# First mixer of a two-layer decoder: the last slice of keys and queries, and the output gates, are made at other places of the recurrence

## The chip, the cores and the metric

The kernel runs on one core of one Trainium2 chip. The metric is device time in microseconds (us) for one execution of the whole program. The engines of the core are PE (matrix products and transposes), DVE, ACT and POOL (elementwise work), and SP, which only issues DMAs; POOL and ACT issue DMAs as well. Each engine works through its own instructions in order and waits on semaphores for the others.

## The reference, cut to what matters

One step of a two-layer decoder. The first layer is an mLSTM mixer over 1104 rows (64 sample rows, 16 meta rows, 1024 prompt rows), each of 1024 features. What the change touches is this mixer:

```python
p = xn @ w_in                        # queries, keys, values, output gate, input and forget gates
q, k, v = heads(p)                   # 8 heads, 64 wide for q and k, 128 wide for v
for chunk in chunks:                 # 9 chunks of rows: the 80 sample and meta rows, then 8 times 128
    s   = (q @ k.T) * exp(decay)
    num = w_inter * (q @ C) + s @ v
    den = w_inter * (q @ n) + sum(s)
    C, n = w_c * C + (w_g * k).T @ v, ...
h   = rmsnorm(num / max(|den|, exp(-m))) * mh_norm
out = (h * sigmoid(og)) @ w_out      # og: the output-gate columns of p
```

After the mixer come a SwiGLU block, the shared keys and values, a second mixer with attention, another SwiGLU block and the final norm. They aren't changed.

## The kernel before, in words

All products are made from two reduced-precision parts of each operand, so that each tile product is three matmuls (L266, L267, L268 in `mm3`). A weight block of 1024 x 128 is loaded raw (512 KB, SP's queue, L323), cast on ACT to its high part (`whi`, L336), and the low part (`wlo`) is the difference, on DVE (L337).

The 1104 rows are held in three slices of 336, 384 and 384 rows (x0, x1, x2; chunks 0-2, 3-5, 6-8). One weight block times one slice is a **unit**: eight **steps** of three matmuls each, into one PSUM bank `mmA` (two buffers). ACT then copies the bank to a staging tile `stg`, and POOL's queue writes it to a scratch tensor in device memory (`qkD` for keys and queries, `ogD` for the output gate).

The mixer, `phase_a`, runs in stages.

1. Values are projected for all rows.
2. `qk_out`: 8 weight blocks times 3 slices make queries and keys. Beside it `rec_prep` makes the decay terms on DVE and ACT; its few transposes on PE are put in after certain units (the ones of `stk` on L909 after the ninth).
3. `recurrence`: the chunks in order. The order of PE, DVE, ACT and POOL is the order of the code there (a manual schedule); SP's order is chosen by the compiler's scheduler. Chunk 0 (the sample rows, each with a state of its own) has many small products (`nps` L1164, `cs` L1213). Each later chunk i has: scores of chunk i+1 (`sps` L1077, `kps` L1083), state (`cp` L1116), decay of chunk i+2 (DVE L1061), outputs (`nps` L1176 and L1180, copied on ACT L1146), and sums of squares of its outputs (ACT L1198). After chunks 2, 5 and 8 `norm_heads` turns the sums into factors and scales the values in place (DVE L1256). A chunk's decay, keys and queries are loaded from scratch memory two chunks ahead (`chunk_load`, POOL's queue), into places that partly lie where chunk 0's states were.
4. Between these products `f(n)` puts n steps of filler on PE. The filler is `gates_out`: 8 weight blocks times 3 slices, 192 steps, whose result passes through a sigmoid on ACT (L741) on its way to `ogD`. What is left of it is emptied at the end of the pass for chunk 6. From then on the filler of chunks 7 and 8 is `gate`: load a gate tile of one head and slice, transpose the head's three value tiles on PE (`ghps` L1272), multiply by gain and gate on DVE (`yg` L1274), and split the product into its two parts (ACT L336, DVE L337). Ten of the 24 are made in the recurrence.
5. `mlp` goes on with the output weights: 8 blocks (`woraw` and `slot` on L520), the first four through one raw place. Then units of the output product (`pops`) alternate with the remaining 14 gates.

The memory of a core is filled from two sides. On the left lie the values, the recurrence's tiles, and the filler's weights; later the output weights lie there. On the right lie the ten `slots` of the feed-forward weights, of which the output weights use some.

Of the kernel before, what the change touches and what calls it, by code (L numbers as in the profile page):

```python
# [16 lines left out]
P = 128  # L17
# [232 lines left out]
class Net:  # L250
# [19 lines left out]
    def consts(self):  # L270
# [13 lines left out]
        self.clast = c.tile([P, 1], F32, name="clast")  # L284
        with self.pool("g0") as gp, self.pool("g0p", space=PSUM) as pp:
# [15 lines left out]
    def load_w(self, pieces, g=None, nk=KT, keep=None):  # L301
# [23 lines left out]
        if g is None:  # L325
# [144 lines left out]
    def mlp(self, H, w, l, heads=None, cb=None):  # L470
# [8 lines left out]
        with self.pool(self.uid("nsp")) as sp, self.pool(self.uid("npp"), bufs=2, space=PSUM) as pn:  # L479
# [26 lines left out]
            with ExitStack() as c:  # L506
# [6 lines left out]
                ws = []  # L513
                for m in range(KT):
# [11 lines left out]
                    self.split(raw, *ws[m])  # L526
                    t = m // 3
                    if m in (1, 4, 7) and (t == 0 or not heads):
                        load(nc.gpsimd if heads else nc.sync, t)

# [11 lines left out]
                if heads:  # L542
                    pad()
                    gate = heads(gp, c.enter_context(self.pool("ghp", bufs=2, space=PSUM)), "gh",
                                 lambda n: self.ny(n)[:, 0])
# [118 lines left out]
def phase_a(self, vt):  # L664
# [6 lines left out]
    with ExitStack() as c3:  # L671
# [29 lines left out]
        self.wpools(c3, 2, 3, side="left")  # L701
        self.cache_prep()

        def qk_out():

            for m in range(8):
                wh, wl = self.load_w([w_in[:, m * P : (m + 1) * P]])
                for t, (t0, t1) in enumerate(TS):
                    n = t1 - t0
                    ps = pp.tile([P, 512], F32, name=self.uid("mmA"), tag="mmA")  # L710
                    self.fm_cols(ps[:, :n], wh, wl, t)
                    s = st.tile([P, SL], F32, name=self.uid("stg"), tag="stg")
                    nc.scalar.activation(s[:, :n], ps[:, :n], AF.Copy, scale=DK ** -0.5 if m < 4 else 1.0)
                    nc.gpsimd.dma_start(qkD[m, :, t0:t1], s[:, :n])
# [10 lines left out]
        def gates_out():  # L725

            get = lambda m: self.load_w([w_in[:, (16 + m) * P : (17 + m) * P]])
            ws = [get(0)]
            for m in range(8):
                wh, wl = ws[m]  # L730
                for t, (t0, t1) in enumerate(TS):
                    n = t1 - t0
                    ps = pp.tile([P, 512], F32, name=self.uid("mmA"), tag="mmA")
                    xh, xl = self.X[t]
                    if t == 1 and m < 7:
                        ws.append(get(m + 1))
                    for k in range(KT):
                        self.mm3(ps[:, :n], wh[:, k, :], wl[:, k, :], xh[:, k, :], xl[:, k, :], k == 0, k == KT - 1)
                        if k == KT - 1:
                            s = st.tile([P, SL], F32, name=self.uid("stg"), tag="stg")  # L740
                            nc.scalar.activation(s[:, :n], ps[:, :n], AF.Sigmoid)  # L741
                            nc.gpsimd.dma_start(ogD[m, :, t0:t1], s[:, :n])
# [4 lines left out]
        def heads(gp, pp, tag="gh", op=None):  # L747
            ready = []
            todo = [(t, h) for t in (0, 1, 2) for h in left[t]]

            def ahead():
                if todo:
                    t, h = todo.pop(0)
                    og = op(self.uid("ogc"))
                    nc.gpsimd.dma_start(og[:, : TS[t][1] - TS[t][0]], ogD[h, :, TS[t][0] : TS[t][1]])
                    ready.append(og)

            def gate(t):
                if not left[t]:
                    return False  # L760
                if not ready:
                    ahead()
                ahead()
                self.gate_head(t, left[t].pop(0), v, ready.pop(0), gp, pp, tag)
                return True
            return gate

        self.recurrence(kp, self.rec, v, qkD, gates_out(), lambda gp: heads(gp, pp, "mmA", lambda n: st.tile([P, SL], F32, name=n, tag="stg")))
# [152 lines left out]
def recurrence(self, kp, rec, v, qkD, fill, gate):  # L921
# [4 lines left out]
    tm, den, ssq = self.fin  # L926

    def f(n):
        for _ in range(n):
            next(fill, None)  # L930

    C = [kp.tile([P, 4, DV + 1], F32, name=f"C{a}") for a in range(3)]
    E = mybir.EngineType
    with ExitStack() as cr, self.pool("recAp", bufs=2, space=PSUM) as pp, \
# [6 lines left out]
        with self.pool("sampA") as sp:  # L941
# [9 lines left out]
            f(2)  # L951
            self.first_sums(R, pp)
            f(3)
# [6 lines left out]
        with self.pool("rec2") as sets[2], self.pool("rec1", bufs=2) as rp, self.pool("rec3") as sets[0], \  # L960
                self.pool("gh0") as gp:
            R, N = N, load(2)
            f(10)
# [3 lines left out]
            g, norm = f, iter(())  # L967
            gate = gate(gp)
# [1640 lines left out]
```

## Time and profile before

| | us |
|---|---|
| median of 3 runs | 2934.68 |
| lowest, highest | 2930.90, 2948.07 |
| the profiled execution: its own time | 2934.39 |
| the profiled execution: span from first to last instruction | 2932.7 |
| PE busy in the span | 2820.7 |
| mean granted clock of PE | 0.988 |

A row of the profile names an engine, a line of the kernel, an operation and its tiles as out<-in; PEld is the loading of weights into PE, which overlaps PE. "Granted clock" is the share of full speed that the throttle allows PE. A row of waits reads: who waited for what, us in total, how often, the longest. In a row by stretch the columns are: start:end and length, then busy us and instructions of PE, PEld, DVE, ACT and POOL, then PE's granted clock, the DMA engines' share, and GB/s. All times of rows are counted from the start of the span.

### The profile page before, as it was taken

How to read it: one execution, taken by the hardware profiler on the slowest of the kernel's cores; microseconds unless marked ns; L12 is line 12 of the kernel's file. 1: busy time of each engine (PE TensorE's matmuls, PEld its weight loads, DVE VectorE, ACT ScalarE, POOL GpSimd, SP SyncE). 2: the span in 40 equal slices, each digit the busy share in tenths (PEclk: the TensorE clock that was granted, in tenths of full speed). 3: DMA queues.
4: the chain of work that ended last, by engine and by line, in shares of the span. 5: the costliest groups of instructions: out<-in, count | busy, mean ns of one | idle time of the engine just before them, and what ended most of it. 6: DMA issues, size and time to landing. Idle time of an engine off the chain costs nothing.

```text
span 2932.7 us, 53641 instructions
## 1 busy us (share of the span) xinstructions
PE 2820.7 (96%) x20542; PEld 2696.2 (92%) x20542; DVE 1704.8 (58%) x3406; ACT 1305.9 (45%) x2591; POOL 1002.1 (34%) x1480
## 2 busy tenths in 40 slices
PE   7999997999999999999999899999999999999998
PEld 7988887999999999999999887777899999999998
DVE  5032456687777755553355443677468777775543
ACT  5122354354444444442344453877444444443432
POOL 2021223156565511114353101454306565641110
PEclk9999998999999999999999999999999999999999
DMA  7052436222222276544443675443412222227652
GB/s 226 7 136 87 132 106 189 79 66 88 74 80 77 84 265 200 190 149 131 148 158 126 207 291 212 150 154 107 146 53 79 76 87 80 79 87 252 215 183 101
DMA packets 300139, 392.79 MB, mean 134 GB/s; under 512 B 32238, under 2 KB 222698, under 8 KB 298858
## 3 DMA queue, kind: packets, MB, share of 16 engines
q1 hardware_dynamic: 262978, 270.05, 28.8%
q0 software_dynamic: 33232, 117.01, 12.0%
q8 instruction: 161, 2.64, 0.4%
q10 hardware_dynamic: 3672, 2.31, 0.3%
q14 instruction: 96, 0.79, 0.1%
HBM read 292.19 MB, written 97.10 MB: 133 GB/s over the span
## 4 chain that ended last, share of the span: by engine, by line
PE 67%; DVE 11%; ACT 4%; issue 4%; DMA 2%; POOL 1%; DVEq 0%; ACTq 0%; POOLq 0%; SPq 0%
PE m L1331 23%; PE dps L266 6%; PE dps L267 6%; PE dps L268 6%; PE tmps L266 3%; PE tmps L267 3%; PE tmps L268 3%; PE sp L2396 1%; DVE slot L337 1%; PE pops L268 1%; PE op L2483 1%; PE pops L266 1%; PE pops L267 1%; DVE s L2400 1%; PE bps L266 1%
## 5 line engine op out<-in xcount | busy, mean ns | idle before, releaser
L337 DVE TENSOR_TENSOR slot<-slot,slot 128x1024 fp32r<-128x1024 f32 (+3 forms) x264 | 268.6, 1020 | 128.8 <-ACT slot L336 122.3
L336 ACT CAST slot<-slot 128x1024 fp32r<-128x1024 f32 (+3 forms) x264 | 207.8, 790 | 235.5 <-PE dps L267 92.0
L1331 PE MATMUL m<-x1h,slot 128*128 128x384 f32 x640 | 177.1, 337 | 1.7 <-DVE Ht L1306 0.8
L1331 PE MATMUL m<-x0h,slot 128*128 128x336 f32 x640 | 167.4, 316 | 0.0
L1331 PE MATMUL m<-x2h,slot 128*128 128x384 f32 x480 | 135.3, 336 | 0.0
L409 POOL TENSOR_TENSOR ns<-ns,nq 128x384 f32<-128x384 f32 (+1 forms) x60 | 63.2, 1053 | 199.4 <-ACT nq L407 197.9
L1438 POOL DMA_DIRECT2D hr<-hT x60 | 32.6, 543 | 285.9 <-DVE T_2l L337 71.0
L108 POOL TENSOR_TENSOR slot<-vA 128x256 f32<-128x256 f32 x80 | 75.5, 955 | 151.9 <-DMA vA<-in_w_gate_up 78.6
L108 POOL TENSOR_TENSOR slot<-Ht 128x256 f32<-128x256 f32 x80 | 75.8, 957 | 150.4 <-DMA Ht<-in_w_gate_up 146.1
L337 DVE TENSOR_TENSOR slot<-vA,slot 128x256 fp32r<-128x256 f32 (+3 forms) x101 | 85.4, 847 | 61.4 <-ACT slot L336 61.4
L337 DVE TENSOR_TENSOR slot<-Ht,slot 128x256 fp32r<-128x256 f32 (+3 forms) x101 | 84.9, 842 | 61.4 <-ACT slot L336 61.4
L1331 PEld LDWEIGHTS m<-x1h,slot 128*128 128x128 f32 x640 | 116.7, 188 | 2.4 <-DVE Ht L1306 1.2
L1331 PEld LDWEIGHTS m<-x0h,slot 128*128 128x128 f32 x640 | 113.4, 188 | 0.0
L1331 PE MATMUL m<-x1l,slot 128*128 128x384 f32 x320 | 107.3, 335 | 0.0
L1331 PE MATMUL m<-x0l,slot 128*128 128x336 f32 x320 | 101.1, 316 | 0.0
L1331 PE MATMUL m<-T_2h,slot 128*128 128x384 f32 x320 | 97.8, 346 | 3.1 <-ACT Ht L1337 1.0
L2423 ACT ACTIVATE s<-s,nb 128x272 f32<-128x272 f32 (+7 forms) x126 | 98.9, 786 | 0.0
L2458 ACT COPY th<-tp 128x768 f32<-128x768 f32 (+1 forms) x80 | 73.5, 920 | 53.6 <-PE tp L2450 30.6
L1331 PE MATMUL m<-T_4h,slot 128*128 128x384 f32 x320 | 96.8, 343 | 0.0
L108 POOL TENSOR_TENSOR Ht<-Ht 128x512 f32<-128x512 f32 (+1 forms) x60 | 84.4, 1408 | 28.4 <-DVE wl1l L337 28.4
L108 POOL TENSOR_TENSOR vA<-vA 128x512 f32<-128x512 f32 (+1 forms) x60 | 84.5, 1409 | 27.4 <-DVE wl0l L337 27.4
L1850 DVE TENSOR_REDUCE ss<-sqb 128x4 f32<-128x256 f32 (+1 forms) x72 | 30.2, 419 | 102.0 <-ACT sqb L1849 101.0
(816 smaller groups left out, 10314.3 us busy)
## 6 DMA issues: line engine op xcount, KB each, us to landing
slot<-in_w_down SPq DMA_DIRECT2D x88, 512.0 KB
wr<-in_w_down SPq DMA_DIRECT2D x42, 512.0 KB
vA<-in_w_gate_up SPq DMA_DIRECT2D x40, 512.0 KB
Ht<-in_w_gate_up SPq DMA_DIRECT2D x40, 512.0 KB
hr<-hT POOLq DMA_DIRECT2D x46, 384.0 KB, 5.2
kp<-in_cache_k SPq DMA_DIRECT2D x32, 512.0 KB
vp<-in_cache_v SPq DMA_DIRECT2D x32, 512.0 KB
wraw<-in_w_in_a SPq DMA_DIRECT2D x24, 512.0 KB
```

Source lines behind the costliest of these rows:

```text
L108: self.net.nc.gpsimd.tensor_tensor(out=o, in0=a, in1=b, op=op)
L266: mm(ps, sh, mh, start=first, stop=False)
L267: mm(ps, sh, ml, start=False, stop=False)
L268: mm(ps, sl, mh, start=False, stop=last)
L336: self.nc.scalar.copy(hi, src)
L337: self.nc.vector.tensor_tensor(out=lo, in0=src, in1=hi.bitcast(F32), op=ALU.subtract)
L409: (nc.vector if x >= late else nc.gpsimd).tensor_tensor(out=s, in0=s, in1=sq, op=ALU.add)
L1331: nc.tensor.matmul(u.b[b][:, :n], w[p][:, k], x[q][:, k], start=new and k == i == 0, stop=k == 1 and i == 2, skip_group_check=True)
L1438: nc.gpsimd.dma_start(hraw[j], hT[t][:, 2 * c : 2 * c + 2])
L1850: nc.vector.tensor_reduce(out=ss[:m, i, :], in_=sq[:m].rearrange("p (h d) -> p h d", d=DH), op=ALU.add, axis=AX.X)
L2423: nc.scalar.activation(ss[z, u], ss[z, u], AF.Exp, bias=nb[:, z : z + 1], accum_out=sm[:, u, z : z + 1])
L2458: nc.scalar.copy(th.rearrange("p x z (u h q) -> p h (x z u) q", h=2, q=64)[:, :, :n], pt[:, :, :n])
```

## The change

- `qk_out` makes slices 0 and 1 only. Slice 2 of keys and queries, 8 units, becomes filler.
- `rest_out` takes the place of `gates_out`: 24 items, first 8 blocks of keys and queries with slice 2, then 8 gate blocks with slices 0 and 1, then the same 8 gate blocks with slice 2. That is 256 steps instead of 192. Weights of keys and queries and of the gate are loaded, cast and split twice. Each item's weights are requested two items ahead; the cast on ACT stands at the start of an item, the subtraction on DVE is put off to the sixth step (`later`).
- The gate goes to `ogD` without sigmoid; the sigmoid is applied to the gate tile after it is loaded again (`heads`). In the recurrence gate tiles are loaded three ahead, the sigmoid goes two ahead, and a gate's split is issued behind the next gate's product (`behind`). The product is written into the gate tile itself.
- Steps per call change: more before chunk 0's parts, 20 instead of 16 in a pass for a later chunk. From the pass for chunk 6 on, each call gives its steps and a gate as well, fifteen gates in all.
- Sums of squares are issued in pieces between other work. The last group's scaling of values (three operations) is moved behind the loads of the first two output weights, and `last_state` behind the loop.
- The filler's weight pool moves from the left side to the right. In `mlp` the raw output weights use places in turn: one on the left, then `slots` 0 and 1. SP's order is fixed there, and DVE's for the first three weights.

```diff
-    def load_w(self, pieces, g=None, nk=KT, keep=None):
+    def load_w(self, pieces, g=None, nk=KT, keep=None, later=None):
...
-        if g is None:
+        if later is not None:
+            nc.scalar.copy(hi, raw)
+            later.append(lambda: nc.vector.tensor_tensor(out=lo, in0=raw, in1=hi.bitcast(F32), op=ALU.subtract))
+        elif g is None:
             self.split(raw, hi, lo)
...
+                first.enter_context(self.tc.manual_schedule(engines={E.PE, E.SP, *([E.DVE] if heads else [])}))
...
-                        raw = wp.tile([P, KT, P], F32, name=self.uid("woraw"), tag="raw", bufs=1) if m < 4 else cut(slots[m % 2])
+                        raw = cut(slots[m % 3 - 1]) if m % 3 else wp.tile([P, KT, P], F32, name=self.uid("woraw"), tag="raw", bufs=1)
...
+                    if m == 1 and heads:
+                        for part in self.late:
+                            part()
...
-                for t, (t0, t1) in enumerate(TS):
+                for t in (0, 1):
...
+        def rest_out():
+
+            plan = [(0, m, (2,), qk_evict) for m in range(8)]
+            plan += [(16, m, (0, 1), og_evict) for m in range(8)]
+            plan += [(16, m, (2,), og_evict) for m in range(8)]
+            later = []
+            get = lambda x: self.load_w([w_in[:, (plan[x][0] + plan[x][1]) * P :][:, :P]], later=later if x > 1 else None)
+            ws = [get(0), get(1)]
+            yield
+            for x, (_, m, ts, evict) in enumerate(plan):
+                wh, wl = ws.pop(0)
+                if x + 2 < len(plan):
+                    ws.append(get(x + 2))
+                for t in ts:
+                    n = TS[t][1] - TS[t][0]
                     ps = pp.tile([P, 512], F32, name=self.uid("mmA"), tag="mmA")
                     xh, xl = self.X[t]
                     for k in range(KT):
                         self.mm3(ps[:, :n], wh[:, k, :], wl[:, k, :], xh[:, k, :], xl[:, k, :], k == 0, k == KT - 1)
                         if k == KT - 1:
+                            evict(m, t, ps)
+                        if k == 5 and later:
+                            later.pop()()
                         yield
...
+                    ready.append([og, lambda: nc.scalar.activation(og, og, AF.Sigmoid)])
...
+        cq.close()
+        self.wpools(c3, 2, 3)
+        rest = rest_out()
+        next(rest)
...
             self.first_queries(R, sp)
-            f(2)
+            f(5)
             self.first_sums(R, pp)
-            f(3)
...
-            f(10)
+            f(8)
             self.chunk_scores(1, R, rp, *args, f)
...
             for i in range(1, NT):
+                if i == 4:
+                    upto(8 * KT)
                 N2 = load(i + 2) if i + 2 < NT else None
                 if i + 1 < NT:
-                    f(3)
+                    f(4 if i > 1 else 8)
+                    some()
                     self.chunk_scores(i + 1, N, rp, *args, f)
...
-                g(2)
+                g(3)
...
-                if i == 6:
-
-                    f(1000)
-                    g = lambda n: gate(0) or gate(1)
+                if i == 5:
+                    ahead()
+                    ahead()
+                    upto(24 * KT)
+                    g = lambda n: f(n) or gate(0) or gate(1)
                 R, N = N, N2
-            for _ in norm:
-                pass
+            rest()
+            next(norm)
+            self.last_state(C[(NT - 1) % 2], nn, rp, pp)
+            next(norm)
+            upto(32 * KT)
...
-            f(4)
+            f(4 if g else 8)
...
-            f(2 if z == 0 else 3)
+            f(3)
...
-        f(1)
+        f(2)
...
-        f(2)
+        f(2 if j else 5)
```

More of the change, by code (lines that the diff above doesn't have):

```diff
@@ L760, in gate @@
                     return False
-                if not ready:
+                while todo and len(ready) < 1 + deep:
                     ahead()
-                ahead()
-                self.gate_head(t, left[t].pop(0), v, ready.pop(0), gp, pp, tag)
-                return True
-            return gate
-        self.recurrence(kp, self.rec, v, qkD, gates_out(), lambda gp: heads(gp, pp, "mmA", lambda n: st.tile([P, SL], F32, name=n, tag="stg")))
+                for x in ready[: deep]:
+                    if len(x) > 1:
+                        x.pop()()
+                part = self.gate_head(t, left[t].pop(0), v, ready.pop(0)[0], pp, tag)
+                if deep > 1:
+                    rest()
+                behind.append(part)
+                if deep == 1:
+                    rest()
+                return True
+            return gate, ahead, rest
+        cq.close()
+        self.wpools(c3, 2, 3)
+        rest = rest_out()
+        next(rest)
+        self.recurrence(kp, self.rec, v, qkD, rest, lambda gp: heads(pp, "mmA", lambda n: gp.tile([P, SL], F32, name=n, tag="og", bufs=4), 2))
     return heads
@@ L981, in recurrence @@
                 next(norm, None)
-                self.chunk_out(i, R, rp, *args, den, ssq, g, exp=N2 and N2["exp"])
+                for _ in squares:
+                    pass
+                squares = self.chunk_out(i, R, rp, *args, den, ssq, g, exp=N2 and N2["exp"])
+                if i % 3 == 2:
+                    for _ in squares:
+                        pass
+                next(squares, None)
                 for _ in norm:
@@ L1258, in norm_heads, with gate_head @@
             op=ALU.mult)
+    parts = [lambda x=x, i=i: part(x, i) for x, i in enumerate(GRP[t])]
+    if t == 2:
+        self.late = parts
+        yield
+    for p in parts:
+        p()
         yield
 @_add(Net)
-def gate_head(self, t, h, v, og, gp, pp, tag):
+def gate_head(self, t, h, v, og, pp, tag):
     nc = self.nc
```

98 lines of the change are left out of this document (60 added, 38 removed).

## The prediction, made before the result was known

> **What bounds the kernel now.** I read the page's busy shares first, then the busy time by stretch over the mixer, then PE's waits there.
>
> ```profile
> PE 2820.7 (96%) x20542; PEld 2696.2 (92%) x20542; DVE 1704.8 (58%) x3406; ACT 1305.9 (45%) x2591; POOL 1002.1 (34%) x1480
> ```
> ```profile
> 190.00:250.00 60.00, 60.00 (x353) 60.00 (x352) 5.37 (x11) 10.16 (x18) 7.58 (x14) 0.97 0.48 113
> 250.00:290.00 40.00, 34.63 (x250) 31.96 (x249) 10.26 (x35) 9.54 (x16) 9.01 (x14) 1.00 0.35 98
> 290.00:326.00 36.00, 34.55 (x165) 27.50 (x167) 15.03 (x44) 8.31 (x23) 3.83 (x8) 0.86 0.34 90
> 326.00:340.00 14.00, 10.64 (x86) 9.58 (x85) 7.92 (x17) 5.01 (x5) 6.38 (x10) 0.88 0.81 215
> 340.00:430.00 90.00, 86.48 (x671) 78.41 (x670) 51.64 (x128) 57.36 (x159) 28.04 (x37) 1.00 0.43 115
> 430.00:465.00 35.00, 22.43 (x172) 18.89 (x173) 15.84 (x35) 10.91 (x36) 11.75 (x20) 0.87 0.40 125
> 465.00:482.00 17.00, 10.42 (x62) 9.96 (x62) 11.58 (x23) 9.45 (x29) 3.21 (x6) 0.80 0.66 189
> 482.00:545.00 63.00, 63.00 (x387) 62.60 (x387) 39.70 (x59) 19.89 (x35) 26.47 (x38) 0.99 0.49 160
> ```
>
> PE is the bound nearly everywhere: 96% of the span. What can be won is the time in which it stands, and that is here. Keys and queries end at about 250, the recurrence runs from there to 465, the output product follows. In the rows, length less PE's busy time is the idle time: 0, 5.4, 1.5, 3.4, 3.5, 12.6, 6.6 and 0 us, together 32.9. Where the clock is below 1, PE's busy time is worth less: busy times (1 - clock) gives 4.8 us at 290, 1.3 at 326, 2.9 at 430 and 2.1 at 465, together 11.1. So PE loses **44 us** between 250 and 482, and none before and after that (the 0.97 before 200 stays as it is). 24.2 of them lie in the last two stretches, 16.4 before 340.
>
> ```profile
> PE ghps L1272 <- DVE yg L1274: 9.1, 4, 6.6
> PE nnp L1004 <- DVE nn L1003: 5.8, 1, 5.8
> PE nps L1176 <- ACT vA L1146: 5.7, 5, 2.2
> PE sps L1077 <- DMA qk<-qkD: 3.4, 1, 3.4
> PE kps L1083 <- DVE eb L1079: 2.3, 2, 1.4
> PE cs L1213 <- DVE km L1209: 2.2, 1, 2.2
> PE nps L1164 <- DVE qm L1159: 1.9, 1, 1.9
> ```
>
> These are PE's waits from 190 to 545. The first two are the end of the recurrence: the filler is used up, a gate is three transposes on PE, and DVE and ACT have much more to do for it. The last four are chunk 0 and the start of chunk 2.
>
> **The change, part by part.** *The move.* Rows of the timeline of PE give a unit's cost:
>
> ```profile
> 198.30 0.34 PE L266 MATMUL mmA<-x2h,whi 128*128 128x384 f32 x1
> ...
> 202.46 0.31 PE L266 MATMUL mmA<-x0h,whi 128*128 128x336 f32 x1
> ```
>
> A unit of slice 2 takes 202.46 - 198.30 = 4.16 us, a step of it 0.52. Eight units, 33.3 us of PE work, leave the stage before 250 and become 64 steps inside the recurrence. PE's work as a whole stays the same. So the gain is what these steps fill of the 44 us, less what new waits cost.
>
> The earlier stage gets shorter by 33.3. The decay preparation beside it must still be covered:
>
> ```profile
> 171.07 1.12 ACT L905 ACTIVATE stk<-bA 8x1104 f32<-8x1104 f32 x1
> ```
> ```profile
> 181.50 0.43 DVE L910 COPY tmA<-tps 80x104 f32<-80x104 f32 x2 [9.19 <-PE tps L909]
> ```
>
> `stk` is complete at 172.2, and its transposes stand behind nine units now as before, at about 180 (three units of 336 rows are traded for two, under 1 us earlier). DVE waited 9.2 us for PE there, so the chain has that much to spare: cost 0.
>
> *The added work.* The sixteen weight blocks that are loaded a second time:
>
> ```profile
> wraw<-in_w_in_a SPq DMA_DIRECT2D x24, 512.0 KB
> ```
> ```profile
> L741 ACT ACT_TABLE_LOAD x11 | 14.1, 1283 | 13.0 <-PE mmA L268 12.8
> L337 DVE TENSOR_TENSOR wlo<-wraw,whi 128x1024 fp32r<-128x1024 f32 x10 | 12.3, 1225 | 75.5 <-ACT whi L336 75.5
> L336 ACT CAST whi<-wraw 128x1024 fp32r<-128x1024 f32 x10 | 10.5, 1047 | 10.3 <-PE mmA L267 10.3
> L741 ACT ACTIVATE stg<-mmA 128x384 f32<-128x384 f32 x16 | 7.9, 492 | 19.7 <-issue 13.1 <-PE mmA L268 6.5
> L1274 DVE SCALAR_TENSOR_TENSOR yg<-ghps,gain,ny 128x384 f32<-128x384 f32 x14 | 8.4, 610 | 0.9 <-DMA ny<-ogD 0.9
> L337 DVE TENSOR_TENSOR x1l<-yg,x1h 128x384 fp32r<-128x384 f32 x8 | 4.6, 593 | 0.6 <-ACT x1h L336 0.6
> L336 ACT CAST x1h<-yg 128x384 fp32r<-128x384 f32 x8 | 4.1, 515 | 1.2 <-DVE yg L1274 1.1
> ```
>
> ACT gets 16 x 1.05 = 16.8 us of casts and 24 sigmoids more (the eviction stays as a copy; at 0.49 each, 11.8), and loses most of eleven table loads (14.1, of which some 5 come back where sigmoid meets exp and sqrt). DVE gets 16 x 1.23 = 19.6 us. SP gets 8.4 MB, which at the 98 to 215 GB/s of these stretches is no bound by itself. All of it lies beside PE while a pass lasts longer than ACT's and DVE's share of it. One pass with `norm_heads` shows that share:
>
> ```profile
> 363.00:379.00 16.00, 15.66 (x127) 13.85 (x127) 11.16 (x28) 11.96 (x30) 3.87 (x6) 1.00 0.49 137
> ```
> ```profile
> 508.18 0.33 PE ghps L1272 x3
> ```
>
> Here 16 steps and the chunk's own products keep PE busy 15.7 of 16 us, DVE 11.2, ACT 12.0. With 20 steps PE has some 17.7. Up to chunk 5 the other two get about two weight blocks more in a pass (2.5 and 2.1 us): DVE 13.7, ACT 14, covered. In the pass for chunk 6 five gates come on top: PE 1.6 (five times 0.33), DVE 5 x (0.61 + 0.59) = 6.0, ACT 5 x (0.49 + 0.52) = 5 and three table loads, 3.8, less one of the eviction's that goes, 1.3. That makes PE 19.3, DVE 19.7 and ACT 12.0 + 2.1 + 5.0 + 3.8 - 1.3 = 21.6. This pass is bound by ACT, **2.3 us** over PE. Chunks 7 and 8 have no decay and no exp left, so there PE is the longest.
>
> The Trainium skill, "ScalarE: Activation LUTs", section "What ACT_TABLE_LOAD costs", states 1283 ns and a drain of about 1380 behind it. Rows of ACT and DVE:
>
> ```profile
> 254.44 1.28 ACT L741 ACT_TABLE_LOAD   x1 [3.18 <-PE mmA L268]
> 255.74 0.45 ACT L741 ACTIVATE stg<-mmA 128x336 f32<-128x336 f32 x1
> 256.08 1.04 ACT L336 CAST whi<-wraw 128x1024 fp32r<-128x1024 f32 x1
> ```
> ```profile
> 257.16 1.23 DVE L337 TENSOR_TENSOR wlo<-wraw,whi 128x1024 fp32r<-128x1024 f32 x1 [26.63 <-ACT whi L336]
> ```
>
> The next activation starts 1.30 us after the load does, so the trace shows no drain behind it. By the page the pass for chunk 6 would lose some 4 us more, and the sum would give 2914.
>
> *250 to 340, 16.4 us lost.* The same rows show where `kps` waits: the subtraction of a weight stands on DVE ahead of chunk 0's decay product, behind a cast behind a table load. The wait on `qm` is of the same kind. The deferral and the missing table load take most of the 1.9 away; I leave 0.5 there, and 1.0 of `kps`' 1.4, since a cast and a subtraction for item 2 still lie ahead. The wait for the first state product (2.2) gets three steps more: 2.2 - 1.56 = 0.6 is left. The wait for chunk 2's keys and queries (3.4) follows from chunk 0's states being stored before their place is loaded again; that stays, and 18 steps lie ahead of it instead of 15: 3.4 - 1.6 = 1.8 left. Of the four waits' 8.9 us, 3.9 stay, so 5.0 are won. The half clock of this part, 6.1 us, came right behind the 2.2 and the 3.4. I take half of it as won, 3.1; bounds 0 and 6.1. Sum **8.1**, bounds 3 and 12.
>
> Against the half: the Trainium skill, "TensorE: Matmul & The Clock Gate", section "HAM oscillation — how this bites in real kernels", states that idle gaps over some 3.4 us re-throttle PE. By that the gap of 2.2 wouldn't matter and 4.8 us would stay: a sum lower by 2.4. The trace has its half clock behind shorter gaps, too.
>
> *340 to 430.* 3.5 lost, mostly single waits for ACT; more steps lie ahead of each, more work on ACT: won 0.
>
> *430 to 482, 24.2 us lost.* Here lay only gates; now 54 steps in three passes (20, 20 and 14) and 10 behind them. `nnp` waited 5.8 since `nn` stood on DVE behind gates and a weight; it is copied early now. `ghps` waited 6.6 for the last norm's chain and a gate behind it; that chain now has 10 steps and the first output units ahead of its use. What comes instead: 2.3 in the pass for chunk 6, and the output weights. By the sizes in the code, their places on the left are those of the chunk tiles of passes 7 and 8, and they can't be loaded before these are free. From the chain of waits:
>
> ```profile
> 454.46 5.97 DMA woraw<-in_w_out_a
> 460.45 1.05 ACT wo L336
> 461.53 1.24 DVE wo L337
> 462.78 5.39 DMA woraw<-in_w_out_a
> ```
>
> A first weight that starts at the very end of the last pass is there 8.3 us later, with 5.2 us of steps (10 x 0.52) and the norm before it; one that starts a pass earlier costs nothing. I take 2, bounds 0 and 6. Two more us for latencies in passes 7 and 8, and 0.5 of clock: 6.8 left, **17.4** won; bounds 9 and 21.
>
> *New waits in the short items.* Eight items of eight steps in chunk 0, each with a cast in ACT's order: ACT stands if a load is late, and `nps` outputs wait behind it. No row shows it; the nearest is the 0 us that fillers wait now and the 8.3 us of a lone load. I take 1, between 0 and 12.
>
> Sum: 8.1 + 0 + 17.4 - 1.0 = 24.5 us. The profiled execution took 2934.4, its span 2932.7, and it lies at the median of 2934.7: **2910 us**.
>
> **The rivals.**
> - *Nearly all is filled.* Clock full throughout, weights there in time: left are 3 to 4 us of waits before 340, 3.5, and 3 at the end. 44 - 10 = 34: 2900. For it: filler of 33.3 us against a hole of 44. Against it: waits on latency, which four more steps shorten and don't remove.
> - *The wait moves to the output weights, DVE and ACT.* First weight 6 late, ACT bound also in pass 7 (3 us), clock halved again (4 us): 11 more are lost: 2921. For it: DVE's and ACT's sums for pass 6 above; POOL and SP in order.
> - *Slower.* Weight loads of the sixteen short items go one after the other, behind SP's waits for chunk 0's stores. Then a block costs 8.3 us as for `woraw`, and 9.6 at the time from issue to landing that chunk loads have:
>
> ```profile
> qk<-qkD POOLq DMA_DIRECT2D x6, 512.0 KB, 7.4
> ```
>
> A short item lasts 8 steps and its share of chunk work, 0.4 of a pass of 17.7 = 7.1. Eight items 2.5 over and eight 1.2 over are 30 us, against 24.5 won: 2940. It decides from 1.5 us per item. Against it: two raw places, and requests two items ahead.
> - *It doesn't do what it says.* The steps move, yet stand at places where PE did not wait, and the earlier stage now waits for its preparation: gain 5, 2929. Against it: the 9.2 us above.
>
> **How the numbers follow.** Forecast 0.46 (its own range 2903 to 2916), nearly all 0.20, output weights and ACT 0.21, slower 0.07, not as said 0.06. To leave out no more than 2 in 10 the range reaches to the two neighbours: **2897 to 2928**. One per cent, 29 us, is about what a measurement of this kernel tells from no change: faster than 2905.3 come the first rival and a third of the forecast, 0.36; slower by as much only the worst of the slower case, 0.03; between them 0.61.
>
> **What would show it.** The stage of keys and queries ends near 217. In the 50 us ahead of the output product PE is busy for over 95% at clock 1. `nnp` waits for nothing, `ghps` under 3 us. The wait for chunk 2's keys is near 1.8. ACT's table loads fall from eleven of L741 to a few for sigmoid. It would be wrong if PE waits for `wo` or ACT waits for `wraw` by more than some us, or if rows behind 545 move.

## The result, and the profile after

The changed kernel took 2923.8 us (median of 13 runs), the kernel before, in as many runs beside it, 2938.5. The ratio is 0.9951, with a 95% interval of 0.994 to 0.9963; the medians differ by 14.6 us. The forecast was 2910, its range 2897 to 2928. So the time lies in the range and 14 us above the forecast, and the steps must be looked at one by one. Three executions of variants below, at 3442, 3799 and 5503 us, lie far above all others and are left out of every median.

The profiled execution took 2928.52 us, with a span of 2926.8. PE's share of the span rose from 96 to 97%. The first view is the page's line of the engines, then the busy time by stretch over the same work as the forecast's rows (length; busy us of PE, PEld, DVE, ACT and POOL; PE's granted clock; DMA share; GB/s), here from the stage of keys and queries to the output product:

```profile
PE 2825.8 (97%) x20542; PEld 2700.4 (92%) x20542; DVE 1721.1 (59%) x3422; ACT 1312.4 (45%) x2620; POOL 1006.0 (34%) x1481
```
```profile
216.00:250.00 34.00, 27.66 (x167) 26.05 (x166) 6.48 (x13) 6.08 (x11) 8.68 (x13) 0.85 0.81 166
250.00:306.00 56.00, 54.21 (x340) 47.09 (x340) 30.01 (x84) 14.99 (x35) 11.45 (x20) 1.00 0.65 167
306.00:390.00 84.00, 83.30 (x651) 76.73 (x647) 45.55 (x107) 39.16 (x130) 26.46 (x37) 1.00 0.59 154
390.00:418.00 28.00, 23.11 (x166) 20.08 (x165) 19.58 (x41) 18.87 (x37) 8.95 (x15) 0.94 0.56 151
418.00:465.00 47.00, 42.18 (x277) 38.46 (x278) 24.60 (x53) 24.68 (x80) 14.46 (x24) 0.93 0.56 170
465.00:532.00 67.00, 65.55 (x400) 64.10 (x399) 38.41 (x56) 26.47 (x46) 25.86 (x36) 1.00 0.50 157
```

Idle time (length less busy) and half clock (busy times what is missing to 1) give, row by row, 10.5, 1.8, 0.7, 6.3, 7.8 and 1.5 us lost: 28.6, where the kernel before lost 44. The middle, 250 to 390, is now nearly full. The first row is the surprise: 10.5 us are lost right at the start of the recurrence, by a wait that the kernel before did not have. PE's waits from 190 to 545 name it:

```profile
PE n0p L1119 <- DMA n<-in_state_n: 6.2, 1, 6.2
PE kps L1152 <- DVE eb L1148: 3.1, 2, 2.4
PE mmA L266 <- ACT stg L748: 2.9, 2, 2.4
PE pops L266 <- ACT wo L340: 1.9, 2, 1.5
PE pops L268 <- DVE wo L341: 1.4, 2, 0.7
PE ghps L1351 <- ACT stg L748: 1.3, 1, 1.3
```

`nnp` and the load of chunk 2's keys are gone from the list, `ghps` fell from 9.1 to 1.7 us in all. New is `n0p`, the transpose of the first normaliser state, which waits for chunk 0's state loads. The timeline of SP in the changed kernel (start, duration, line, transfer) shows why these were late:

```profile
218.24 0.36 SPq L1091 DMA_DIRECT2D qk<-qkD  x1
...
220.14 7.13 SPq L1110 DMA_DIRECT2D C<-in_state_C  x8
227.32 3.81 SPq L1112 DMA_DIRECT2D n<-in_state_n  x4
```

SP's own waits and, for comparison, SP's timeline in the kernel before:

```profile
SPq L1091 <- DMA qkD<-stg: 17.2, 1, 17.2
```
```profile
189.06 6.96 SPq L1041 DMA_DIRECT2D C<-in_state_C  x8
196.07 1.89 SPq L1043 DMA_DIRECT2D n<-in_state_n  x4
204.83 24.39 SPq L323 DMA_DIRECT2D wraw<-in_w_in_a  x3
245.33 0.37 SPq L1022 DMA_DIRECT2D qk<-qkD  x1
```

Before, the states left at 189 and the load of chunk 0's keys and queries came last. After, that load stands ahead: it waits 17.2 us for the stores of the stage, and twelve state loads stand behind it. What that costs on PE is seen in PE's timeline of the changed kernel:

```profile
230.23 0.34 PE L268 MATMUL mmA<-x2h,wlo 128*128 128x384 f32 x1
236.77 0.28 PE L1119 MATMUL n0p<-ident,n 32*128 32x32 f32 x1 [6.20 <-DMA n<-in_state_n]
236.98 1.98 PE L1185 MATMUL cp<-vA,kw 16*64 16x129 f32 x16
...
240.02 0.52 PE L266 MATMUL mmA<-x2h,whi 128*128 128x384 f32 x1
240.34 0.52 PE L267 MATMUL mmA<-x2l,whi 128*128 128x384 f32 x1
...
244.72 0.34 PE L266 MATMUL mmA<-x2h,whi 128*128 128x384 f32 x1
244.89 0.34 PE L267 MATMUL mmA<-x2l,whi 128*128 128x384 f32 x1
```

Six us of waiting, and then products that start every 0.32 us instead of every 0.17, until 244.7: by the row's clock (27.66 us busy at 0.85) some 4 us more.

The second surprise lies outside the mixer. From the first product of keys and queries to the last gate's, the mixer took 382.7 us before and 366.0 after, 16.7 less; the profiled executions differ by only 5.9. The rest was lost in stages whose code did not change. Rows of PE's groups by shape, 20 to 135 us (the value projection; count, busy us, mean ns of one), before and after:

```profile
L266 PE MATMUL tmps<-whi,x1h 128*128 128x256 f32 x72 | 19.9, 276 | 0.0
L267 PE MATMUL tmps<-wlo,x0h 128*128 128x256 f32 x48 | 13.5, 281 | 0.0
```
```profile
L266 PE MATMUL tmps<-whi,x1h 128*128 128x256 f32 x72 | 20.4, 283 | 0.0
L267 PE MATMUL tmps<-wlo,x0h 128*128 128x256 f32 x48 | 13.5, 281 | 0.0
```

A product with slice 1 (or 2) of the activations as its stationary part (the one that PEld loads) takes 281 to 283 ns instead of 276, at a granted clock of 1.00 in both; one with slice 0 takes the same as before. From the first `tmps` to the first product of keys and queries that is 123.7 us after and 120.4 before; in the second mixer, from `fgps` to `og0ps`, 265.3 after and 258.6 before. Together 10 us.

### The profile page after: what moved, and what is told of

It is laid out like the page before. It is cut to its first block, busy times and chain, and to the rows that moved or that the text cites. A ratio compares the mean times of both kernels' runs of the same rounds, so it can differ in the third digit from the quotient of the medians.

```text
span 2926.8 us, 53724 instructions
## 1 busy us (share of the span) xinstructions
PE 2825.8 (97%) x20542; PEld 2700.4 (92%) x20542; DVE 1721.1 (59%) x3422; ACT 1312.4 (45%) x2620; POOL 1006.0 (34%) x1481
## 4 chain that ended last, share of the span: by engine, by line
PE 74%; DVE 11%; issue 5%; DMA 5%; ACT 4%; POOL 1%; SPq 0%; DVEq 0%; ACTq 0%; POOLq 0%
PE m L1410 23%; PE dps L267 6%; PE dps L266 6%; PE dps L268 6%; PE tmps L268 4%; PE tmps L266 4%; PE tmps L267 4%; PE mmA L266 2%; PE mmA L267 2%; DVE slot L341 2%; PE mmA L268 2%; PE sp L2475 2%; PE op L2562 1%; DVE s L2479 1%; PE bps L266 1%
```

## The experiments

All ratios are to the kernel before on the same chip, in runs beside it. "Mixer" is the length from the first product of keys and queries to the last gate's, read from PE's rows of the one profiled execution. The last column names the first wait of PE, with its length, that the kernel before did not have. The variants ran on different chips, so they are best compared by their ratios.

| kernel | median us | ratio, 95% | mixer | PE's first new wait |
|---|---|---|---|---|
| before, two profiles | 2937 to 2941 | 1 | 382.7, 393.1 | |
| the change, two profiles | 2923.8, 2924.9 | 0.995 (0.994 to 0.997) | 366.0, 365.4 | states 6.2, 6.6 |
| states_first | 2930.1 | 0.996 (0.9947 to 0.9973) | 371.4 | queries 13.7 |
| samp_right | 2925.5 | 0.9955 (0.9943 to 0.9968) | 364.3 | states 5.9 |
| samp_right_first | 2930.2 | 0.9975 (0.9966 to 0.9984) | 370.6 | queries 13.4 |
| pool_left | 2925.4 | 0.996 (0.9945 to 0.9974) | 367.0 | first weight 5.6 |
| split2 | 2928.1 | 0.9947 (0.9927 to 0.9968) | 364.0 | states 8.0 |
| split2_first | 2917.5 | 0.9916 (0.9893 to 0.9939) | 353.3 | none |
| split2_half | 2923.7 | 0.9934 (0.9912 to 0.9957) | 360.1 | none |
| slice2_back | 2943.8 | 1.0008 (0.9994 to 1.0023) | 383.7 | states 4.8 |
| no_sigmoid | 2926.1 | 0.9957 (0.9943 to 0.9971) | 366.7 | states 5.6 |
| gates_from_7 | 2930.7 | 0.9974 (0.9963 to 0.9985) | 367.6 | states 6.4 |

### The two kernels once more

No edit.

> The changed kernel itself, once more, as the measure for the other runs on this chip. Ratio to the kernel before: 0.995, as measured (2924 against 2938). In the first profile of it the rows outside the mixer were longer than in that of the kernel before: 4 us ahead of 142 and 6 us between 1380 and 1613, so that the mixer alone had gained 16.7 us. If that belongs to the single execution, it is gone in this profile and the span shrinks by some 5 to 10 us; if it belongs to the kernel (the rival: places in memory that moved), the same stretches are as long again. The 6.2 us wait for the first normaliser state and the half clock behind it should stand at the same place in either case.

> The kernel before, once more. In its first profile the rows outside the mixer were 4 to 10 us shorter than in the profiles of the changed kernel and of its variants, in which the first unit of keys and queries starts between 139.3 and 142.2, against 138.1. If that is a matter of the single execution, this profile has them as long as the others do (the first unit at 139 to 142, and the mixer from its first unit to its last gate 383 us long, as in the first profile); if it belongs to the kernel, the first unit starts at 138 again and the rows behind are short again.

The ratio repeated, 0.9953. The value projection and the second mixer's projections took 123.8 and 265.3 us in the changed kernel's second profile, 120.4 and 258.7 in that of the kernel before. So this loss belongs to the kernel and not to the single execution. All twelve profiles with the change, in which pools, orders and gates of the mixer were varied, have 123.0 to 123.8 and 265.2 to 265.3. That it comes of places in memory, as the rival says, no run shows.

The mixer of the kernel before, on the other hand, differed by 10 us between its two profiles (382.7 and 393.1), at the same waits: `nnp` 5.8 in both, the first state product 2.2 in both. One row of the second profile:

```profile
290.00:326.00 36.00, 33.89 (x133) 26.21 (x134) 15.83 (x47) 5.02 (x7) 2.02 (x5) 0.72 0.25 69
```

The clock was 0.72 here and 0.86 in the first profile: 9.5 us lost instead of 4.8, behind the same wait of 2.2. Over all the forecast's rows from 250 to 545 the idle time is the same, 33.2 us against 32.9, and the half clock costs 22.2 instead of 11.8: that is the whole 10. A profile of the kernel before is thus good to some 10 us, and the one that the forecast was made against was among the short ones: 2934.4, 4 us under the median of 2938.5 of the larger count of runs.

### The state loads: order and place

The first idea was the order alone:

```diff
-            R = self.chunk_load(0, r0, *args)
-            N = dict(eb=...)
             self.first_load(R, sp)
+            R.update(self.chunk_load(0, r0, *args))
+            N = dict(eb=...)
```

> Chunk 0's twelve state loads are issued ahead of its load of keys and queries instead of behind it. Theory: in the changed kernel these loads stood in SP's order behind the load of the queries, which waits 17 us for their stores; with them ahead, PE's wait of 6.2 us for the first normaliser state and the half clock behind it (10 us at about 0.57 = some 4 us) go: 9 to 10 us less than the changed kernel, about 2914, ratio to before about 0.992. Rival: the loads are late because the transfers themselves share the DMA engines with the first filler weights and not because of the order; then they leave early, land late, and no more than 2 us are won. Second rival: the weights behind them are late in turn, and PE waits for those: within 2 us of the changed kernel.

It failed: no gain, rather 5 us more. SP's waits, then PE's:

```profile
SPq L1111 <- PE mmA L268: 18.8, 1, 18.8
```
```profile
PE sps L1147 <- DMA qk<-qkD: 13.7, 2, 13.2
```

With the state loads ahead, SP waited 18.8 us at them, for the last product of the stage with a weight's low half; then the queries stood behind the states, and PE waited 13.2 us for those. So the states had a second reason to be late: their place. The change closes the stage's weight pool and lays chunk 0's tiles where it was. By sizes in the code the stage's pool has 2 raw blocks, 3 high and 3 low halves of 4096 bytes a partition, 32768; chunk 0's own set takes 16384 of that, the small tiles ahead of the states 13440; so the states begin 2944 bytes below the end of the stage's pool, on a low half that is in use until the stage's last product. In the kernel before the pool stayed open for the filler, and the chunk tiles lay beyond it.

Moving the short-lived tiles to the other side of the memory, without and with the order:

```diff
-        with self.pool("sampA") as sp:
+        with self.pool("sampA", side="right") as sp:
```

> The tiles of chunk 0's states (and its other short-lived ones) are placed on the right side of the memory, where no weight of the keys and queries lay; SP's order stays that of the changed kernel, with the state loads behind the load of the queries. With the states loaded first but at the old place, SP waited 18.8 us for PE's last product of the stage instead of 17.2 for the stores. Theory (order and place each hold the loads back, and either is enough): the load of the queries still blocks SP until 218, the states leave at 220, PE waits some 6 us for the normaliser: within 2 us of the changed kernel, 2923 to 2927. Rival (the place alone was the cause, and the order follows it): 9 to 10 us less, about 2915.

> Both at once: the states' tiles on the right, and their loads ahead of that of the queries in SP's order. Theory: they leave at about 198, land beside the last units of the stage, the load of the queries leaves at 218 as in the changed kernel, and PE's 6.6 us for the normaliser and the half clock behind it go: 8 to 10 us less, 2915 to 2917, ratio to before 0.992. Rival (2.3 MB of transfers that start 20 us earlier delay the weights of the stage, or the queries wait as long): PE's wait moves to the first scores or to weights, and the time is within 3 us of the changed kernel.

samp_right came out as its theory said (2925.5), samp_right_first did not: SP again waited 18.8 us for the stage's last product, and PE 13.4 for the queries. The place had moved and, by that wait, was still taken (by my working from the sizes over 1280 bytes instead of 2944, which no run shows).

The filler's pool on the left again:

```diff
-        self.wpools(c3, 2, 3)
+        self.wpools(c3, 2, 3, side="left")
```

> The filler's weights lie on the left again, as in the kernel before, all else as changed. SP's order then has the state loads ahead of that of the queries, and the states' place is no longer that of the stage's weights. Theory: at the start it gains what both changes of place and order gain, 8 to 10 us; at the end the output weights fall on places that the filler's weights hold until the last step, and PE waits for them as the kernel with the last slice taken back did, 7 us, against 3 now: 2918 to 2922. Rival (the places matter at neither end): 2923 to 2927.

The states leave at 188.6 and PE's wait for them is gone; instead it waits as long for the filler's first weight:

```profile
PE mmA L266 <- ACT whi L340: 5.6, 1, 5.6
```

SP's timeline of this kernel has the reason:

```profile
215.79 0.40 SPq L1091 DMA_DIRECT2D qk<-qkD  x1
216.29 14.15 SPq L324 DMA_DIRECT2D wraw<-in_w_in_a  x5
```

Now it is the filler's weights that stand behind the load of the queries, which again waits for its stores; they leave at 216.3, when the stage is about to end. At the end of the recurrence the output weights cost 2.6 us, not the 7 of my theory. The time, 2925.4, is that of the changed kernel, not the 2918 to 2922 of my theory: the order had only put another load in the place of the states. Wanted is a version in which states and first weights both leave ahead of the queries, and which has room for them. The stage's products take 8 us for a weight block now (two units) and its cast and subtraction 2.3, so two pairs of halves should do where three were kept. split2 has this edit alone, split2_first that of the order as well:

```diff
-        self.wpools(cq, 2, 3, side="left")
+        self.wpools(cq, 2, 2, side="left")
```

> The weights of the keys' and queries' stage get two pairs of high and low halves instead of three, 8 KB of a partition less. By the sizes in the code, the first state tile began 16384 (chunk 0's own set) and 13440 bytes (smaller tiles) above the start of the stage's pool of 32768 bytes, so its first 2944 bytes lay on the top low half, that of the last unit; on the right side they overlapped still by 1280. With a pool of 24576 bytes they overlap nothing of it. The order of SP stays that of the changed kernel. Theory (order and place each hold the state loads back): the load of the queries blocks SP until 218 still, PE waits some 6 us for the normaliser, time within 2 us of the changed kernel, 2923 to 2927. Rival (the place was all of it): about 2915. Second rival (two pairs are too few for the stage): PE waits for weights ahead of 217, slower by more than 3 us.

> Two pairs of halves as above, and the state loads ahead of that of the queries. Theory: now nothing holds them but the end of the decay preparation at 190; they leave ahead of 200 and have landed when the stage ends, the load of the queries leaves near 218, PE's 6 to 6.6 us for the normaliser and the half clock behind it go: 8 to 10 us less than the changed kernel, 2915 to 2917, ratio to before 0.992. Rival (2.1 MB of states beside the weights make those late, or the load of the queries lands late, as it did at 235 where the states held SP): PE's wait moves to the first scores, and the time is 2922 to 2930.

Both came out nearly as the theory said (2923 to 2927 and 2915 to 2917). With the place free and the order old, PE waits 8.0 us for the states; with both, SP's timeline reads:

```profile
197.63 9.24 SPq L1111 DMA_DIRECT2D C<-in_state_C  x8
206.92 1.72 SPq L1113 DMA_DIRECT2D n<-in_state_n  x4
...
216.53 0.39 SPq L1092 DMA_DIRECT2D qk<-qkD  x1
```

and the start of the recurrence, by stretch:

```profile
216.00:250.00 34.00, 33.58 (x237) 32.13 (x237) 13.36 (x35) 10.23 (x17) 8.89 (x14) 1.00 0.70 178
250.00:296.00 46.00, 44.18 (x274) 37.19 (x273) 26.45 (x71) 12.06 (x29) 10.81 (x18) 1.00 0.63 160
```

PE is busy for 33.58 of 34 us at full clock, against 27.66 at 0.85. The median is 2917.5, 10.6 less than split2 on the same chip; the mixer is 12.7 us shorter than the changed kernel's. The theory had 8 to 10. The six runs lie in two groups, three at 2912 to 2913 and three at 2922, and the profile is of the fastest, so the size is known to some 7 us either way, by the interval of its ratio; but all six lie below the six of split2 (2924.5 to 2930.0). This is the version that beats both kernels: 0.9916 to the kernel before.

### The moved steps

```diff
-                for t in (0, 1):
+                for t in (0, 1, 2):
...
-            plan = [(0, m, (2,), qk_evict) for m in range(8)]
-            plan += [(16, m, (0, 1), og_evict) for m in range(8)]
+            plan = [(16, m, (0, 1), og_evict) for m in range(8)]
...
-    done = [0]
+    done = [8 * KT]
```

> The last slice of the keys and queries is made in the earlier stage again, as in the kernel before; the gates by slices, their pipeline and the places stay as changed. Theory (the moved steps are what fills PE's idle time at the end of the recurrence): 33.3 us of steps are missing in the last passes again, the recurrence ends in gates and norms alone, PE loses some 15 to 20 us more there, and the late state loads cost nothing, since the stage ahead is long enough to cover them (10 us back): 2929 to 2935, ratio 0.997 to 1.0. Rival (the gain comes from the gates by slices and their pipeline, not from the moved steps): 2915 to 2924, as the changed kernel or better by the state loads.

All of the gain is gone, and some 9 us more than I thought: 2943.8, ratio 1.0008, 19 us over the changed kernel on the same chip. The gates by slices and their pipeline alone gain nothing in this form, in which 20 steps a pass use up the filler early. PE's waits at the end of this kernel:

```profile
PE ghps L1350 <- DVE ogc L1352: 10.4, 5, 3.6
PE pops L266 <- ACT wo L340: 7.2, 1, 7.2
PE kps L1151 <- DVE eb L1147: 5.4, 2, 4.6
```

Without the moved steps the first output weight is 7.2 us late and the gates stand bare. And the state loads cost 4.8 us here too, which my theory had excluded: here as well they stand behind the load of the queries, which leaves at 248.5, and then wait 3.5 us for a last product of the stage.

### The end of the recurrence

A plain copy of the same size at the sigmoid's place, which leaves the sigmoid out:

```diff
-                    ready.append([og, lambda: nc.scalar.activation(og, og, AF.Sigmoid)])
+                    ready.append([og, lambda: nc.scalar.copy(og, og)])
```

> The sigmoid of the gates is left out: a plain copy of the same size stands at its place, so that ACT does as many passes over the data but loads no tables for it. Theory (the pass for chunk 6 is bound by ACT, with its five table loads of 1.28 us, 6.4 us): PE's waits at 402 and 415 of the changed kernel, 2.7 us each, shrink to below 1, 3 to 5 us less than the changed kernel. Rival (these waits are latencies of a chain through DVE, with the decay and the norm scaling ahead): less than 1.5 us. The wait for the first states stays in both.

By its time the rival was right: 2926.1, mixer 366.7 against 366.0 and 365.4. The table loads went, from five in this pass to two, and the waits stayed; only their releaser changed, from ACT's eviction to DVE's gate product. PE's waits of this kernel behind 380:

```profile
PE mmA L266 <- DVE ogc L1353: 3.5, 2, 2.6
PE kps L1152 <- DVE eb L1148: 3.1, 1, 3.1
```

So it isn't ACT's tables that set this pass. The rows of the changed kernel show two different chains. The first wait, before 405.23, goes through a gate tile. Its load stands on POOL's queue behind a store that waited for ACT's eviction, and takes 6.65 us from issue to landing (by the chain of waits), where the median of these loads is 3.0; ACT then waits for it, and PE's bank is emptied on ACT behind it:

```profile
395.24 6.65 DMA ogc<-ogD
```
```profile
401.92 0.48 ACT L788 ACTIVATE ogc<-ogc 128x336 f32<-128x336 f32 x1 [1.48 <-DMA ogc<-ogD]
```
```profile
405.23 0.69 PE L266 MATMUL mmA<-x2h,whi 128*128 128x384 f32 x1 [2.35 <-ACT stg L748]
```

Without the sigmoid ACT comes to that place earlier and waits longer for the same load:

```profile
398.77 0.47 ACT L788 COPY ogc<-ogc 128x336 f32<-128x336 f32 x1 [3.98 <-DMA ogc<-ogD]
```

The second wait, of `kps` before 418.2, does stand on DVE, where the norm and a weight's subtraction are ahead of the scores' product:

```profile
412.88 3.50 DVE L1329 TENSOR_TENSOR vA<-vA,fA 128x1024 f32<-128x1024 f32 x3
416.29 1.22 DVE L328 TENSOR_TENSOR wlo<-wraw,whi 128x1024 fp32r<-128x1024 f32 x1
417.43 1.28 DVE L1148 TENSOR_TENSOR eb<-sps,eb 128x512 f32<-128x512 f32 x2
```

No variant loads the gate tiles earlier, so what that load alone costs is not measured. Then fewer gates in this pass, none (gates_from_7, on the changed kernel) or three (split2_half, on split2_first) instead of five:

```diff
-                if i == 5:
+                if i == 5:
+                    upto(24 * KT)
+                if i == 6:
                     ahead()
                     ahead()
-                    upto(24 * KT)
                     g = lambda n: f(n) or gate(0) or gate(1)
```

> Gates start one pass later, with chunk 7 instead of chunk 6, so that the pass for chunk 6 has its 20 steps of filler alone. Theory (five gates in the pass for chunk 6 are too much for ACT and DVE, as forecast with 2.3 us): the waits at 402 and 415 go, with the half clock behind them, 3 to 6 us less than the changed kernel, 2919 to 2922. Rival (these waits are of DVE's norm and decay chain, and the gates that are put off pile up in the passes behind): the waits move, within 2 us of the changed kernel, or some us over it.

```diff
-                    g = lambda n: f(n) or gate(0) or gate(1)
+                    turn = [0]
+
+                    def g(n):
+                        f(n)
+                        turn[0] += 1
+                        if turn[0] > 5 or turn[0] % 2:
+                            gate(0) or gate(1)
```

> As the kernel above, and in the pass for chunk 6 a gate comes at every second place instead of at each, three instead of five. Theory (the waits of that pass, 2.7 and 3.1 us with half clock behind them, come from too many gates in it, and with none of them in it the waits at the end grew by 8 us): between the two, 2 to 3 us less than the kernel above. Rival (the gates are needed by the output product at a fixed time, so each put off is paid there): within 1.5 us of the kernel above.

In gates_from_7 the pass for chunk 6 became full, and the two passes behind paid for it:

```profile
390.00:418.00 28.00, 27.65 (x218) 25.19 (x218) 20.95 (x43) 16.49 (x40) 11.03 (x16) 1.00 0.64 172
418.00:465.00 47.00, 35.33 (x234) 32.37 (x232) 23.70 (x45) 25.82 (x72) 10.73 (x19) 0.92 0.55 169
```

4.5 us of PE's time were won in the first of these rows and 6.9 lost in the second; the ratio, 0.9974, is that of some 6 us over the changed kernel. split2_half has a mixer 6.8 us longer than split2_first and a median 6.1 higher, but its runs (2916.7 to 2930.3) overlap those of split2_first; that it gains 2 to 3 us, as my theory had it, is not seen, and that it loses is not sure. Both fit gates that are wanted early: what is put off is paid for in the passes behind. That they would pay still earlier, in the pass for chunk 5, was not tried.

## Why the prediction was right, and where it was not

Taken against the two first profiles, the forecast's sum was 24.5 us in the mixer and nothing outside. What was measured: 15.4 by the rows by stretch (44 - 28.6), 16.7 by the mixer's length, less 10 outside; 5.9 between the executions. The medians differ by 14.6, since the profile before was 4 us short of its median and the profile after 5 over its own. Step by step the misses are larger than the 14 us: the state loads took 9.4 more than forecast, the end won 8.8 less and the projections lost 10; against that the rows ahead of 430 won 9.2 more, and the profile after lies 4.7 over its median. That these misses cancel so far that the time lies in the range is in part luck.

- **The move** fills what the rows said, and the mechanism holds: taken back, the whole gain goes (slice2_back). The stage's last product starts at 218.97, with a start that is 4 us later than in the profile before (142.1 against 138.1); forecast "near 217". The decay preparation stayed covered: PE's waits for `tps` are 0.8 us in all. (Of the nine units ahead of these transposes five are of 336 rows now and three were before, not two for three; the effect, under 1 us, is as forecast.)
- **250 to 340**: forecast 8.1 won. Without the states' wait 14.5 were won (16.4, less the 1.8 of the row 250:306 and 0.1 of the first): the deferral and the added steps together took away nearly all of what I left there, and the half clock went with the gaps; no run parts the two. split2_first shows it alone: 0.4 and 1.8 us lost in its first two rows.
- **340 to 430**: forecast 0, won 2.8; the row 306:390 loses 0.7.
- **New waits in the short items** was the step that failed: 1.0 was taken, about 10.4 came. My bounds of 0 to 12 held the size, but the mechanism wasn't in the text. I looked at the weights that the items load and at ACT's order; I did not follow SP's queue for what stands behind the load of chunk 0's queries, and did not work out which tile lies where the closed pool had been. The closed pool stands in the diff; SP's order is the compiler's, and in the code the queries' load is written ahead of the states'. Either of the two alone holds the states back: order mended (states_first), place mended (split2), nothing is won; both mended, 10.6 between medians.
- **430 to 482**: forecast 17.4 won, 6.8 left; measured 15.6 left (6.3, 7.8 and 1.5), so 8.6 won, just under my lower bound of 9. The term for the pass for chunk 6, 2.3, was put on ACT with its table loads (three were forecast, five came); with three of the five taken away nothing changes. The pass waits for a gate tile's late load and then for DVE's norm and subtraction, and it costs 6.3 with its half clock. The output weights took 3.3 (1.9 and 1.4) where I had 2. PE was to be busy for over 95% at clock 1 in the last 50 us; the row 418:465 has 90% at 0.93.
- **Rows behind 545 do not move**: wrong, and not only there. 10 us were lost in the two projections with a 256-wide moving part, one of them ahead of 142. The sum had these stages at nothing, since their code stays.

The half clock again: the forecast held the row against the Trainium skill, "TensorE: Matmul & The Clock Gate", section "HAM oscillation — how this bites in real kernels", which has PE re-throttled by gaps over some 3.4 us. Here the gap of 2.35 us that ends at 405.2 is enough, by the changed kernel's rows of the next four us (the clock was 1.00 from 398 to 405):

```profile
405.00:407.00 2.00, 1.77 (x6) 1.77 (x7) 0.47 (x2) 1.93 (x4) 1.07 (x2) 0.50 0.72 183
407.00:409.00 2.00, 2.00 (x13) 1.91 (x12) 0.88 (x2) 0.04 (x1) 0.00 (x0) 0.64 0.85 288
```

Of the rivals, the one with 2921 was nearest by its number; its mechanisms came in part only, the output weights half as late as it had them, and a gate's load and DVE instead of ACT. The slower case did not come: a short item's weights were there in time. But its picture, loads held up behind SP's wait for chunk 0's stores, was right for another load.

What stays open: why products with stationary slices 1 and 2 take longer. Their loads into PE do not, by their rows: means of 188 to 190 ns in both kernels. The change adds one 96-byte tile ahead of the activations, so that these lie 96 bytes further in all stages; that fits the fact that untouched stages changed and that all twelve variants have it alike. No kernel was run that moves the activations alone, so it is a guess. If the 10 us could be had back, split2_first would come to about 2908, an estimate from these rows.

## What to carry to other kernels

When work is moved out of a stage that covered something, list every transfer that was issued under it, and ask of each two things: what waits ahead of it in its queue, and whose place it takes. Both had to be mended here, and mending one alone made nothing faster. And compare the stages that a change does not touch: here 10 us were given back in two of them.

## What the runs showed of the hardware

- The same products at the same clock took 276 or 281 to 283 ns, by the kernel and not by the execution; in two profiles against twelve the two projections differ by 10 us of 2924.
- Behind the same wait of 2.2 us the half clock lasted differently in two executions of one kernel: a clock of 0.86 and of 0.72 over 36 us, and 10 us in the mixer over all such places. The two profiles of the changed kernel, with fewer gaps, have mixers of 366.0 and 365.4; that filled gaps take away the scatter is not shown, since the six runs of split2_first lie in two groups 9 us apart.
